# Dealing layer 2's projections to the attention groups in other shares, and summing the shift's part of their biases in layer 1

## Chip, cores and metric

The kernel runs on one core of one Trainium2 chip. The metric is device time in microseconds (us) of one execution, the median of several runs. Shown beside it is one profiled execution, from which every row below is taken.

## What is computed

A model of two layers on 2048 tokens of width 1024 in float32. Layer 1 is gated linear attention (4 heads, chunks). Layer 2 is stick-breaking attention with 16 heads of 64 (8 pairs of heads here) and causal blocks. What enters a projection is normed and modulated: a scale and a shift per channel, both computed from the vector `c`.

```
x = x + gate * gla_mixer(rms_norm(x) * (1 + scale) + shift)              # layer 1
hk = rms_norm(x, kv_gain) * (1 + kv_scale) + kv_shift                    # layer 2
k, v = split(hk @ w_kv)
h = rms_norm(x, norm_gain[1]) * (1 + scale) + shift
q, g = split(h @ sb_w_in)
z = q @ k.T * scale                                                      # per head, s < t only
weights = exp(log_sigmoid(z) + sum over s' in (s, t) of log_sigmoid(-z)) # stick breaking
x = x + gate * ((weights @ v) * silu(g)) @ w_out
y = rms_norm(x)
```

The shift is constant over the tokens, so `shift @ w` is one number per output column, a bias: `bias[f] = sum over d of shift[d] * w[d, f]`.

## The kernel before

Tokens stand in four groups of 512 (`g`). Every matmul operand that needs more than one pass is split into a rounded part (`hi`) and a rest (`lo`); a projection step (`mm3`, L143) is three matmuls of 128x512, and the four projections of one pair and group (`pair_linear`, L732: v, k, q and gate, tiles `lv`, `lk`, `lq`, `lg`) are 33 steps, about 32 x 3 matmuls.

Layer 1 (`layer0`, L661) goes over the groups; side generators started with `spawn` advance one step every so many main steps. The raw halves of all weights, 512 KB each, go through the pool `wraw` of three buffers; ScalarE rounds them (`wh_`), VectorE makes the rest (`wl_`).

Layer 2 (`layer1`, L932) goes over the 8 pairs `p`, and in each over the four groups. Group `g` attends to `g + 1` blocks in two heads, so it has 8, 16, 24 and 32 attention steps. In one step TensorE makes scores `z` (L821, L822); ScalarE a sigmoid `S` (L825); VectorE a running product over `S` (a scan, L830); five steps later TensorE transposes `S` into one of two PSUM banks `pt` (L838); ScalarE and VectorE split it into `sh` and `sl` (L841, L842), which frees the bank; two steps on TensorE multiplies it with the values (`o`, L855, L856). The first four steps of each head are on the diagonal, with narrower tiles.

TensorE's order is the order of the code; the other engines are ordered by a scheduler with priorities, and each then runs its queue in that order. Between attention steps, `step(fill, at)` (L956) advances the projections: during group `g` those of group `g + 1` of the same pair, during the last group those of the next pair's group 0, always 33 steps spread evenly over the stage:

```
elif g + 1 < NG:
    fill.append([pair_linear(p, g + 1, Ws[p], Ls[p]), LIN_STEPS, 0, 1, 0])
```

The weights of the next pair are scaled in `load_scaled` (L121), whose last instructions add the raw weights, times the shift, into `wacc` (L138, L140): 2 x 8 VectorE instructions for a pair. `pair_bias` (L720) sums `wacc` over the partitions with matmuls against ones (`pb`, L725) and copies the result (`wbias`).

Of the kernel before, what the change touches and what calls it, by code (L numbers as in the profile page):

```python
# [34 lines left out]
def yoco_kernel(ctx: ExitStack, tc: tile.TileContext, I: dict, O: dict):  # L35
# [624 lines left out]

    def layer0():  # L661
# [4 lines left out]
        for g in range(NG):  # L666
# [7 lines left out]
            spawn(after, 10, 2)  # L674
            mix, gat = spawn(heads(T)), spawn(gates(T))
# [16 lines left out]
            run(slow)  # L692
            after = normed_out(T)
# [26 lines left out]
    def pair_bias(p, W, i):  # L720
        if W.bias[i] is None:
            pb = bank(pl, f"pb_{p}_{i}")
            W.bias[i] = m2.tile([P, 2], F32, tag="wbias", name=f"wbias_{p}_{i}", bufs=4)
            for j in range(2):
# [3 lines left out]
        return W.bias[i][:, 0:1], W.bias[i][:, 1:2]  # L728
# [3 lines left out]
    def pair_linear(p, g, W, Ls):  # L732
# [14 lines left out]
        bk, bv = pair_bias(p, W, 0)  # L747
# [25 lines left out]
        bq, bgt = pair_bias(p, W, 1)  # L773
# [150 lines left out]

    Ws = {}
# [6 lines left out]
    def layer1(after):  # L932
# [30 lines left out]

        for p in range(SBP):
            for g in range(NG):
# [107 lines left out]
```

## Time and profile before

| what | value |
|---|---|
| median of 3 runs | 2706.71 us (2704.65 to 2706.72) |
| the profiled execution, device time | 2703.88 us |
| its span, first to last instruction | 2702.1 us |
| TensorE (PE) busy | 2607.2 us, 96% |
| weight loads (PEld) busy | 2184.4 us, 81% |
| VectorE (DVE) busy | 2110.4 us, 78% |
| ScalarE (ACT) busy | 1517.6 us, 56% |
| mean granted TensorE clock | 0.989 |

PE's busy time counts each matmul until a modelled end, although the next has begun: the rows of two matmuls in a row overlap. The distance between the starts of two rows is what one really takes. Layer 1 fills the first 976.1 us; pairs 1 to 6 repeat the stages of pair 2, which lie at 1363.6 us (group 0), 1395.5 (1), 1435.1 (2) and 1489.9 to 1556.7 (3). In pair 7 the last group, from 2456.7 us, is filled with the output projection.

### The profile page before, as it was taken

How to read it: one execution, taken by the hardware profiler on the slowest of the kernel's cores; microseconds unless marked ns; L12 is line 12 of the kernel's file. 1: busy time of each engine (PE TensorE's matmuls, PEld its weight loads, DVE VectorE, ACT ScalarE, POOL GpSimd, SP SyncE). 2: the span in 40 equal slices, each digit the busy share in tenths (PEclk: the TensorE clock that was granted, in tenths of full speed). 3: DMA queues.
4: the chain of work that ended last, by engine and by line, in shares of the span. 5: the costliest groups of instructions: out<-in, count | busy, mean ns of one | idle time of the engine just before them, and what ended most of it. 6: DMA issues, size and time to landing. Idle time of an engine off the chain costs nothing.

```text
span 2702.1 us, 38165 instructions
## 1 busy us (share of the span) xinstructions
PE 2607.2 (96%) x14040; PEld 2184.4 (81%) x14040; DVE 2110.4 (78%) x2933; ACT 1517.6 (56%) x2677; POOL 167.4 (6%) x358
## 2 busy tenths in 40 slices
PE   5999999999999999999999999999999999999998
PEld 4888888888788878788787887887887887887887
DVE  7647767676675658978979969979879789789866
ACT  4746756574485445545545645546556555556644
POOL 3000000000000011000010010010000010010000
PEclk7999999999999999999999999999999999999999
DMA  6326445545732463342243334243243243323464
GB/s 246 118 74 209 151 151 175 168 148 173 232 131 72 164 247 127 106 145 90 96 146 116 114 107 154 88 137 116 75 148 110 72 151 113 115 93 117 148 212 147
DMA packets 116682, 371.91 MB, mean 138 GB/s; under 512 B 13872, under 2 KB 18096, under 8 KB 116496
## 3 DMA queue, kind: packets, MB, share of 16 engines
q1 hardware_dynamic: 116496, 369.47, 40.8%
q8 instruction: 111, 1.82, 0.3%
q14 instruction: 75, 0.61, 0.1%
HBM read 311.75 MB, written 40.89 MB: 131 GB/s over the span
## 4 chain that ended last, share of the span: by engine, by line
PE 75%; DVE 17%; ACT 3%; issue 3%; DMA 1%; POOL 0%; SPq 0%; DVEq 0%; POOLq 0%; ACTq 0%
PE pt L838 7%; DVE S L830 5%; PE z L822 4%; PE o L856 4%; PE z L821 4%; PE o L855 3%; DVE sl L842 3%; PE pg L150 2%; PE pg L152 2%; PE pg L151 2%; PE pf L150 2%; PE pf L151 2%; PE pf L152 2%; PE py L150 2%; PE lk L150 2%
## 5 line engine op out<-in xcount | busy, mean ns | idle before, releaser
L841 ACT ACTIVATE sh<-pt 128x512 fp32r<-128x512 f32 (+3 forms) x640 | 341.5, 534 | 531.7 <-PE pt L838 522.1
L842 DVE SCALAR_TENSOR_TENSOR sl<-pt,sh 128x512 fp32r<-128x512 f32 (+3 forms) x640 | 384.0, 601 | 163.5 <-ACT sh L841 157.6
L830 DVE TENSOR_TENSOR_SCAN S<-S,S 128x512 f32<-128x512 f32 x384 | 489.5, 1275 | 3.4 <-ACT S L825 3.0
L838 PE MATMUL pt<-ident,S 128*128 128x128 f32 x2176 | 346.9, 275 | 34.7 <-DVE sl L842 34.2
L838 PEld LDWEIGHTS pt<-ident,S 128*128 128x128 f32 x2176 | 266.1, 141 | 119.7 <-DVE sl L842 33.0
L825 ACT ACTIVATE S<-z 128x512 f32<-128x512 f32 (+3 forms) x640 | 339.5, 531 | 12.6 <-PE o L856 4.6
L821 PE MATMUL z<-k,q 128*128 128x512 f32 (+3 forms) x640 | 284.4, 444 | 0.0
L822 PE MATMUL z<-k,ql 128*128 128x512 f32 (+3 forms) x640 | 234.1, 366 | 0.9 <-DVE sl L842 0.5
L856 PE MATMUL o<-sl,v 128*128 128x512 f32 (+3 forms) x640 | 234.2, 366 | 0.0
L855 PE MATMUL o<-sh,v 128*128 128x512 f32 (+3 forms) x640 | 230.6, 360 | 0.0
L830 DVE TENSOR_TENSOR_SCAN S<-S 128x128 f32<-128x128 f32 (+3 forms) x256 | 209.3, 820 | 19.7 <-POOL S L827 16.7
L827 POOL TENSOR_SCALAR_AFFINE_SELECT S<-S 128x128 f32<-128x128 f32 x256 | 86.1, 337 | 1251.1 <-ACT S L825 1232.2
L444 PE MATMUL pv<-wh_v,h 128*128 128x256 f32 x512 | 155.0, 303 | 0.0
L446 PE MATMUL pv<-wh_v,h 128*128 128x256 f32 x512 | 145.3, 284 | 0.0
L445 PE MATMUL pv<-wl_v,h 128*128 128x256 f32 x512 | 145.2, 284 | 0.0
L855 PEld LDWEIGHTS o<-sh,v 128*128 128x128 f32 x640 | 120.6, 188 | 27.2
L856 PEld LDWEIGHTS o<-sl,v 128*128 128x128 f32 x640 | 120.6, 189 | 25.7
L821 PEld LDWEIGHTS z<-k,q 128*128 128x128 f32 x640 | 121.8, 190 | 5.5
L822 PEld LDWEIGHTS z<-k,ql 128*128 128x128 f32 x640 | 123.1, 192 | 1.5 <-DVE sl L842 0.7
L150 PE MATMUL pg<-h,wh_g 128*128 128x512 f32 x256 | 112.6, 440 | 0.0
L150 PE MATMUL lk<-xb,wh_w_kv 128*128 128x512 f32 x256 | 102.5, 400 | 7.6 <-DVE oB L869 7.6
L150 PE MATMUL lv<-xb,wh_w_kv 128*128 128x512 f32 x256 | 102.9, 402 | 3.5 <-DMA xb<-xn 3.5
(266 smaller groups left out, 6350.3 us busy)
## 6 DMA issues: line engine op xcount, KB each, us to landing
xb<-xn SPq DMA_DIRECT2D x256, 512.0 KB, 5.0
wa_l<-in_w_ada_dram SPq DMA_DIRECT2D x40, 512.0 KB, 5.2
wr_f<-in_w_out_dram SPq DMA_DIRECT2D x40, 512.0 KB, 3.8
x<-in_x_dram SPq DMA_DIRECT2D x32, 512.0 KB, 6.5
wr_v<-in_w_v_dram SPq DMA_DIRECT2D x32, 512.0 KB, 4.5
wr_kq<-in_w_kq_dram SPq DMA_DIRECT2D x32, 512.0 KB, 4.1
wr_g<-in_w_g_dram SPq DMA_DIRECT2D x32, 512.0 KB, 3.9
wr_out<-in_w_out_dram SPq DMA_DIRECT2D x32, 512.0 KB, 3.8
```

The lines of the kernel that those rows point to most:

```text
L150: nc.tensor.matmul(out, hi, x[kt][0], start=first and i == 0, stop=False)
L444: nc.tensor.matmul(o, xh, hi, start=i == 0, stop=False)
L446: nc.tensor.matmul(o, xl, hi, start=False, stop=i == len(steps) - 1)
L821: nc.tensor.matmul(z, L.q[:, h, tcol], k[:, h, 0:w], start=True, stop=False)
L822: nc.tensor.matmul(z, L.ql[h][:, tcol], k[:, h, 0:w], start=False, stop=True)
L825: nc.scalar.activation(s, z, AF.Sigmoid, scale=-SCALE_B)
L830: nc.vector.tensor_tensor_scan(s[:, ::-1], s[:, ::-1], s[:, ::-1], 1.0 if diag else self.before.S[tb][:, 0:1], ALU.mult, ALU.min)
L838: nc.tensor.transpose(pt[:, tb * P:(tb + 1) * P], self.S[tb][:, sb * P:(sb + 1) * P], ident)
L841: nc.scalar.activation(hi, pt[:, t0 * P:], AF.Copy, bias=-1.0)
L842: nc.vector.scalar_tensor_tensor(lo, pt[:, t0 * P:], -1.0, hi.bitcast(F32), op0=ALU.add, op1=ALU.subtract)
L855: nc.tensor.matmul(o, v, hi, start=self.diag and sb == 0, stop=False)
L856: nc.tensor.matmul(o, v, lo, start=False, stop=self.c == 0 and sb == 3)
```

## The change

First, the bias sums move. `load_scaled` loses its sums; the new `bias_sums` runs as a side generator in layer 1 (group index 2 for `w_kv`, 3 for `w_qg`), one half of a weight every 12 main steps. It loads all raw weights of all pairs once more, sums them on VectorE, transposes each sum (`pb`) and adds over the free axis into one small tile `biases`. Second, the projections become one stream over all pairs and groups, in the same order; a group's stage now gets its share by `AHEAD`: after group `g`, the stream is that part of a projection ahead of what the next group needs. Within a pair the stages get 16.5, 29.7, 38 and 47.9 steps, where each had 33. The scaling of the next weights hangs on the stream: `w_qg` of a pair along its own group 0, `w_kv` along the second half of group 3 of the pair before.

```
-                s = b[:, kt:kt + 1]
-                with relaxed(400):
-                    if kt == 0:
-                        nc.vector.tensor_scalar(acc, raw[:, j], s, None, op0=ALU.mult)
-                    else:
-                        nc.vector.scalar_tensor_tensor(acc, raw[:, j], s, acc, op0=ALU.mult, op1=ALU.add)
                 yield
...
+    biases = cpool.tile([P, 4 * SBP], F32, tag="biases", name="biases")
+    def bias_sums(i):
+        which, m = (("w_kv", "kvm"), ("w_qg", "l1m"))[i]
+        b = mods[m][1]
+        def total(p, acc):
+            pb = bank(po, f"pb_{i}_{p}")[:, 0:2 * P]
+            for j in range(2):
+                nc.tensor.transpose(pb[:, j * P:(j + 1) * P], acc[:, j * P:(j + 1) * P], ident)
+            at = 4 * p + 2 * i
+            nc.vector.tensor_reduce(biases[:, at:at + 2], pb.rearrange("p (j t) -> p j t", j=2),
+                                    axis=mybir.AxisListType.X, op=ALU.add)
+        before = None
+        for p in range(SBP):
+            acc = t2(f"bs_{i}_{p}")[:, 0:2 * P]
+            for hf in range(2):
+                raw = wraw.tile([P, 4, 256], F32, tag="wraw", name=f"wb_{i}_{p}_{hf}")
+                nc.sync.dma_start(raw, I[which][p][:, 4 * hf:4 * hf + 4, :])
+                for j in range(4):
+                    kt = 4 * hf + j
+                    s = b[:, kt:kt + 1]
+                    with relaxed(200):
...
+                yield
+            if before:
+                total(*before)
+            before = p, acc
+        yield
+        total(*before)
...
             spawn(after, 10, 2)
+            extra = spawn(bias_sums(g - 2), 10, 12) if g > 1 else iter(())
...
             run(slow)
+            run(extra)
...
-    def pair_bias(p, W, i):
-        if W.bias[i] is None:
-            pb = bank(pl, f"pb_{p}_{i}")
...
-                nc.tensor.matmul(pb[:, j:j + 1], W.acc[:, i, j * P:(j + 1) * P], ones,
-                                 start=True, stop=True)
-            nc.vector.tensor_copy(W.bias[i], pb[:, 0:2])
+    def pair_bias(p, i):
+        at = 4 * p + 2 * i
+        return biases[:, at:at + 1], biases[:, at + 1:at + 2]
...
+    AHEAD = (0.1, 0.0, 0.15, 0.6)
...
+        def projections():
+            for p in range(SBP):
+                for g in range(NG):
+                    side, start, every = iter(()), 0, 2
+                    if g == 0:
+                        if p == 0:
+                            continue
+                        side = pair_weights(p, Ws[p], 1)
+                    elif g == NG - 1 and p + 1 < SBP:
+                        Ws[p + 1] = new_weights(p + 1)
+                        side, start = pair_weights(p + 1, Ws[p + 1], 0), LIN_STEPS // 2
+                    for i, _ in enumerate(pair_linear(p, g, Ws[p], Ls[p])):
+                        if i >= start and (i - start) % every == 0:
+                            next(side, None)
+                        yield
+                    run(side)
+                    yield
+        stream = projections()
+        made = [0]
+        def project(n):
+            while made[0] < n and next(stream, 0) is None:
+                made[0] += 1
...
-                elif g + 1 < NG:
-                    fill.append([pair_linear(p, g + 1, Ws[p], Ls[p]), LIN_STEPS, 0, 1, 0])
...
+                n0, n1 = made[0], int(LIN_STEPS * (NG * p + g + 1 + AHEAD[g]))
...
+                def go(at):
+                    step(fill, at)
+                    project(n0 + int(at * (n1 - n0) + 1e-6))
...
+                project(LIN_STEPS * (NG * p + g + 1))
```

How TensorE's queue changes, in pair 2, group 3, first head: from one pair of scores to the next. Before (one step of three matmuls of the next pair's `lk`):

```order
L150 MATMUL lk_3_0_13865<-xb_3_0_1_13653,wh_w_kv3_0_13359 128x512
L151 MATMUL lk_3_0_13865<-xb_3_0_1_13653,wh_w_kv3_0_13359 128x512
L152 MATMUL lk_3_0_13865<-xb_3_0_1_13653,wl_w_kv3_0_13360 128x512
L855 MATMUL o_2_3_0_3_13850<-sh_2_3_0_3_1_13814,v2_2_3_13594 128x384
L856 MATMUL o_2_3_0_3_13850<-sl_2_3_0_3_1_13815,v2_2_3_13594 128x384
L838 MATMUL pt_2_3_0_2_0_13889<-ident_86,S_2_3_0_2_0_13759 128x128
L838 MATMUL pt_2_3_0_2_0_13889<-ident_86,S_2_3_0_2_1_13782 128x128
L838 MATMUL pt_2_3_0_2_0_13889<-ident_86,S_2_3_0_2_2_13802 128x128
L838 MATMUL pt_2_3_0_2_0_13889<-ident_86,S_2_3_0_2_3_13821 128x128
```

After, the same place; a second projection step stands between the values and the transposes (in every second attention step there), and the stream has reached `lq`:

```order
L142 MATMUL lq_3_0_14081<-xb_3_0_1_13797,wh_w_qg3_0_13817 128x512
L143 MATMUL lq_3_0_14081<-xb_3_0_1_13797,wh_w_qg3_0_13817 128x512
L144 MATMUL lq_3_0_14081<-xb_3_0_1_13797,wl_w_qg3_0_13818 128x512
L879 MATMUL o_2_3_0_3_14085<-sh_2_3_0_3_1_14038,v2_2_3_13749 128x384
L880 MATMUL o_2_3_0_3_14085<-sl_2_3_0_3_1_14039,v2_2_3_13749 128x384
L142 MATMUL lq_3_0_14081<-xb_3_0_2_13799,wh_w_qg3_0_13817 128x512
L143 MATMUL lq_3_0_14081<-xb_3_0_2_13799,wh_w_qg3_0_13817 128x512
L144 MATMUL lq_3_0_14081<-xb_3_0_2_13799,wl_w_qg3_0_13818 128x512
L862 MATMUL pt_2_3_0_2_0_14108<-ident_86,S_2_3_0_2_0_13979 128x128
L862 MATMUL pt_2_3_0_2_0_14108<-ident_86,S_2_3_0_2_1_14001 128x128
L862 MATMUL pt_2_3_0_2_0_14108<-ident_86,S_2_3_0_2_2_14026 128x128
L862 MATMUL pt_2_3_0_2_0_14108<-ident_86,S_2_3_0_2_3_14045 128x128
```

VectorE's queue in pair 2, group 2, second head, off the diagonal. Before:

```order
L830 SCALAR_TENSOR_TENSOR S_2_2_1_1_0_13433<-S_2_2_1_1_0_13433,S_2_2_1_2_0_13319 128x512
L140 SCALAR_TENSOR_TENSOR wacc_3_13028<-wr_w_kv3_1_13519,cond_kv_2178,wacc_3_13028 128x256
L140 SCALAR_TENSOR_TENSOR wacc_3_13028<-wr_w_qg3_0_13712,cond_l1_4112,wacc_3_13028 128x256
L842 SCALAR_TENSOR_TENSOR sl_2_2_0_0_3_13450<-pt_2_2_0_0_3_13444,sh_2_2_0_0_3_13449 128x512
L830 SCALAR_TENSOR_TENSOR S_2_2_1_1_1_13456<-S_2_2_1_1_1_13456,S_2_2_1_2_1_13348 128x512
L140 SCALAR_TENSOR_TENSOR wacc_3_13028<-wr_w_kv3_1_13519,cond_kv_2178,wacc_3_13028 128x256
L140 SCALAR_TENSOR_TENSOR wacc_3_13028<-wr_w_qg3_0_13712,cond_l1_4112,wacc_3_13028 128x256 x2
L842 SCALAR_TENSOR_TENSOR sl_2_2_1_2_0_13473<-pt_2_2_1_2_0_13467,sh_2_2_1_2_0_13472 128x512
```

After, the sums are gone from between the scan and the split; the projection's own `ql` stand there earlier than they did, and four scalings of the next weights' rest in a row:

```order
L854 SCALAR_TENSOR_TENSOR S_2_2_1_1_0_13632<-S_2_2_1_1_0_13632,S_2_2_1_2_0_13528 128x512
L802 SCALAR_TENSOR_TENSOR ql0_2_3_13636<-lq_2_3_13501,biases_124,q_2_3_13635 64x512
L804 SCALAR_TENSOR_TENSOR ql1_2_3_13637<-lq_2_3_13501,biases_124,q_2_3_13635 64x512
L866 SCALAR_TENSOR_TENSOR sl_2_2_0_0_3_13667<-pt_2_2_0_0_3_13661,sh_2_2_0_0_3_13666 128x512
L854 SCALAR_TENSOR_TENSOR S_2_2_1_1_1_13673<-S_2_2_1_1_1_13673,S_2_2_1_2_1_13556 128x512
L866 SCALAR_TENSOR_TENSOR sl_2_2_1_2_0_13689<-pt_2_2_1_2_0_13683,sh_2_2_1_2_0_13688 128x512
L854 SCALAR_TENSOR_TENSOR S_2_2_1_1_2_13695<-S_2_2_1_1_2_13695,S_2_2_1_2_2_13581 128x512
L131 SCALAR_TENSOR_TENSOR wl_w_qg3_1_13959<-wr_w_qg3_1_13956,a_l1_6169,wh_w_qg3_1_13958 128x256 x4
L866 SCALAR_TENSOR_TENSOR sl_2_2_1_2_1_13713<-pt_2_2_1_2_1_13708,sh_2_2_1_2_1_13712 128x384
```

VectorE's queue in layer 1, group 2, at the first weight half of the sums, after (before, none of the rows of L680 and L682 stood there):

```order
L680 TENSOR_SCALAR bs_0_0_4209<-wb_0_0_0_4210,cond_kv_2179 128x256
L117 TENSOR_TENSOR wl_v2_1_1_4292<-wr_v2_1_1_4289,wh_v2_1_1_4291 128x1024
L391 TENSOR_SCALAR gk_2_1_4248<-u_2_1_4246,vecs_97 128x512
L196 TENSOR_TENSOR ss_y1_4207<-ss_y1_4207,sq_y1_1_4228 128x512
L682 SCALAR_TENSOR_TENSOR bs_0_0_4209<-wb_0_0_0_4210,cond_kv_2179,bs_0_0_4209 128x256
L196 TENSOR_TENSOR ss_y1_4207<-ss_y1_4207,sq_y1_2_4243 128x512
L682 SCALAR_TENSOR_TENSOR bs_0_0_4209<-wb_0_0_0_4210,cond_kv_2179,bs_0_0_4209 128x256
L449 TENSOR_TENSOR gk_2_0_4132<-pk_2_0_4295,gk_2_0_4132 128x512
```

The sums of one half are spread among other work of the queue, and the raw half stays in its `wraw` buffer until the last of its four.

## Rows read from the trace of the kernel before

**Rows 1.** The page, part 1: engine, busy us, share of the span, instructions.

```profile
PE 2607.2 (96%) x14040; PEld 2184.4 (81%) x14040; DVE 2110.4 (78%) x2933; ACT 1517.6 (56%) x2677; POOL 167.4 (6%) x358
```

**Rows 2.** Stretches, pair 2: us, then PE, PEld, DVE, ACT, POOL busy, clock, DMA.

```profile
1363.60:1395.50 31.90, 31.90 (x164) 26.57 (x162) 17.72 (x24) 12.00 (x24) 3.70 (x10) 1.00 0.25 70
1395.50:1435.10 39.60, 39.60 (x213) 33.25 (x212) 32.25 (x44) 20.39 (x41) 4.06 (x10) 1.00 0.50 168
1435.10:1489.90 54.80, 51.99 (x281) 42.40 (x279) 51.72 (x81) 34.82 (x71) 3.71 (x10) 1.00 0.34 115
1489.90:1556.70 66.80, 64.40 (x356) 53.33 (x353) 64.86 (x88) 39.77 (x78) 3.57 (x10) 1.00 0.32 106
```

**Rows 3.** Waits of PE in pair 2: us in total, times, longest.

```profile
PE pt L838 <- DVE sl L842: 4.0, 7, 1.2
PE lk L150 <- DVE oB L869: 1.1, 1, 1.1
```

**Rows 4.** Waits of PE from 976.1 to 2456.7 us.

```profile
PE pt L838 <- DVE sl L842: 31.5, 53, 2.3
PE lk L150 <- DVE oB L869: 7.6, 7, 1.1
```

**Rows 5.** Timeline of PE, pair 2, group 2: start, us, instruction, idle before.

```profile
1481.18 0.40 PE L856 MATMUL o<-sl,v 128*128 128x512 f32 x1
1482.74 0.30 PE L838 MATMUL pt<-ident,S 128*128 128x128 f32 x1 [1.17 <-DVE sl L842]
```

**Rows 6.** Timeline of DVE there.

```profile
1482.04 0.56 DVE L842 SCALAR_TENSOR_TENSOR sl<-pt,sh 128x384 fp32r<-128x384 f32 x1
1482.51 0.48 DVE L140 SCALAR_TENSOR_TENSOR wacc<-wr_w_qg,cond_l,wacc 128x256 f32<-128x256 f32 x1
1482.90 1.28 DVE L830 TENSOR_TENSOR_SCAN S<-S,S 128x512 f32<-128x512 f32 x1
1484.10 0.66 DVE L869 TENSOR_TENSOR oB<-o,ot 64x512 f32<-64x512 f32 x1
```

**Rows 7.** Timeline of PE, pair 2, early in group 3.

```profile
1507.04 0.39 PE L152 MATMUL lv<-xb,wl_w_kv 128*128 128x512 f32 x1
1507.28 0.38 PE L838 MATMUL pt<-ident,S 128*128 128x128 f32 x2
1507.41 0.48 PE L821 MATMUL z<-k,q 128*128 128x512 f32 x1
1507.73 0.39 PE L822 MATMUL z<-k,ql 128*128 128x512 f32 x1
...
1508.42 0.50 PE L725 MATMUL pb<-ones,wacc 128*128 128x1 f32 x4
1510.05 0.50 PE L150 MATMUL lk<-xb,wh_w_kv 128*128 128x512 f32 x1 [1.13 <-DVE oB L869]
```

**Rows 8.** DVE groups by line, 976.1 to 2456.7: busy us, mean ns | idle before.

```profile
L780 DVE SCALAR_TENSOR_TENSOR ql<-lq,wbias,q 64x512 fp32r<-64x512 f32 x31 | 23.5, 757 | 0.9
L140 DVE SCALAR_TENSOR_TENSOR wacc<-wr_w_qg,cond_l,wacc 128x256 f32<-128x256 f32 x49 | 23.4, 477 | 0.8
...
L727 DVE COPY wbias<-pb 128x2 f32<-128x2 f32 x14 | 1.9, 136 | 0.0
```

**Rows 9.** Busy time by stretch, layer 1: groups 2 and 3.

```profile
498.30:730.30 232.00, 228.57 (x1281) 195.33 (x1280) 164.98 (x223) 140.32 (x211) 3.86 (x4) 0.99 0.53 176
730.30:976.10 245.80, 245.63 (x1339) 208.24 (x1340) 146.79 (x224) 134.54 (x212) 4.23 (x6) 0.99 0.41 140
```

**Rows 10.** Waits of the DMA queue on SP from 498.3 to 976.1 us, the longest.

```profile
SPq L106 <- DVE wl_out L117: 66.9, 13, 12.0
```

**Rows 11.** The page, part 6: DMA issues, KB each, us to landing.

```profile
wr_v<-in_w_v_dram SPq DMA_DIRECT2D x32, 512.0 KB, 4.5
```

**Rows 12.** DVE groups by line, layer 1, group 2.

```profile
L117 DVE TENSOR_TENSOR wl_out<-wr_out,wh_out 128x1024 fp32r<-128x1024 f32 x8 | 9.8, 1219 | 2.4 <-ACT wh_out L116 2.4
```

More of the change, by code (lines that the diff above doesn't have):

```diff
@@ L119, in load_split, with load_scaled @@
         return out
-    def load_scaled(name, src, out, mod, acc):
-        a, b = mod
+    def load_scaled(name, src, out, a):
         for hf in range(2):
@@ L659, in is_ready @@
         yield
+    biases = cpool.tile([P, 4 * SBP], F32, tag="biases", name="biases")
[19 more added lines that the diff above has]
+                    with relaxed(200):
+                        if kt == 0:
+                            nc.vector.tensor_scalar(acc, raw[:, j], s, None, op0=ALU.mult)
+                        else:
+                            nc.vector.scalar_tensor_tensor(acc, raw[:, j], s, acc, op0=ALU.mult, op1=ALU.add)
+                yield
[4 more added lines that the diff above has]
+        total(*before)
     def layer0():
@@ L709, in new_weights @@
         W = Piece()
-        W.acc = t2(f"wacc_{p}").rearrange("p (i f) -> p i f", i=2)
-        W.w, W.bias = {}, [None, None]
+        W.w = {}
         return W
@@ L717, in pair_weights @@
         W.w[which] = []
-        return load_scaled(f"{which}{p}", I[which][p], W.w[which], mods[m], W.acc[:, i])
-    def pair_bias(p, W, i):
-        if W.bias[i] is None:
-            pb = bank(pl, f"pb_{p}_{i}")
-            W.bias[i] = m2.tile([P, 2], F32, tag="wbias", name=f"wbias_{p}_{i}", bufs=4)
-            for j in range(2):
-                nc.tensor.matmul(pb[:, j:j + 1], W.acc[:, i, j * P:(j + 1) * P], ones,
-                                 start=True, stop=True)
-            nc.vector.tensor_copy(W.bias[i], pb[:, 0:2])
-        return W.bias[i][:, 0:1], W.bias[i][:, 1:2]
+        return load_scaled(f"{which}{p}", I[which][p], W.w[which], mods[m][0])
+    def pair_bias(p, i):
+        at = 4 * p + 2 * i
+        return biases[:, at:at + 1], biases[:, at + 1:at + 2]
     LIN_STEPS = 4 * KT + 1
@@ L746, in pair_linear @@
         yield from mm3(pv, W.w["w_kv"], 1, xs)
-        bk, bv = pair_bias(p, W, 0)
+        bk, bv = pair_bias(p, 0)
         vt = t2(f"vt_{n}")
@@ L772, in pair_linear @@
         yield from mm3(pq, W.w["w_qg"], 0, xs)
-        bq, bgt = pair_bias(p, W, 1)
+        bq, bgt = pair_bias(p, 1)
         L.q = t4(f"q_{n}", [P, 2, TG], F32R)
@@ L975, in layer1 @@
                     fill.append([finals, FINAL_STEPS + SBP - 1, 0, 1.0, 0])
-                elif g + 1 < NG:
-                    fill.append([pair_linear(p, g + 1, Ws[p], Ls[p]), LIN_STEPS, 0, 1, 0])
-                elif p + 1 < SBP:
-                    fill.append([pair_weights(p + 1, Ws[p + 1], 1), KT, 0, 0.6, 0])
-                    fill.append([pair_linear(p + 1, 0, Ws[p + 1], Ls[p + 1]), LIN_STEPS, 0, 1, 0])
-                if g == 2 and p + 1 < SBP:
-                    Ws[p + 1] = new_weights(p + 1)
-                    fill.append([pair_weights(p + 1, Ws[p + 1], 0), KT, 0.5, 1, 0])
+                n0, n1 = made[0], int(LIN_STEPS * (NG * p + g + 1 + AHEAD[g]))
                 steps = [(u, j) for u in units for j in range(4)]
+                def go(at):
+                    step(fill, at)
+                    project(n0 + int(at * (n1 - n0) + 1e-6))
                 for i, (u, j) in enumerate(steps):
@@ L987, in layer1 @@
                     turns.append((u, j))
-                    step(fill, (i + 0.7) / len(steps))
+                    go((i + 0.7) / len(steps))
                     if len(values) > LAG_V:
@@ L991, in layer1 @@
                         v[0].values(v[1])
-                    step(fill, (i + 1) / len(steps))
+                    go((i + 1) / len(steps))
                     if len(turns) > LAG_T:
```

## Prediction

> **What bounds the kernel now.** The page comes first, and it misleads: TensorE is busy 96% of the span [rows 1], so nothing seems to be left but TensorE's own work, of which this change removes next to nothing. The second view is the busy time by stage in one pair of layer 2 [rows 2]. There the reader is to see two regimes. In groups 0 and 1 TensorE is never idle and VectorE is busy 56% and 81% of the stage. In groups 2 and 3 VectorE is busy 94% and 97%, and TensorE loses 2.8 and 2.4 us. The third view says to whom [rows 3]: in each pair seven transposes wait for `sl`, the VectorE instruction that frees a `pt` bank, 4.0 us, and one `lk` waits 1.1 us for a PSUM bank until `oB` is done. Over pairs 0 to 7, up to the start of the last group, that is 53 times and 31.5 us, and 7 times and 7.6 us [rows 4]; 7 x 7 of the 53 are pairs 0 to 6.
>
> The idle column is too small. In [rows 5] the value matmul starts at 1481.18 and the transpose that waits at 1482.74, 1.56 us later; a matmul of this size otherwise gives way after 0.24 us (from 1507.04 to 1507.28 in [rows 7]). The loss is 1.32 us, and the row says 1.17: some 0.16 us of each such wait lies under the modelled end of the matmul ahead. So a pair loses 4.0 + 7 x 0.16 + 1.1 = 6.2 us.
>
> Why `sl` is late stands in VectorE's queue [rows 6]: a sum into `wacc` runs ahead of a 1.28 us scan, and holds the queue from 1482.51 to 1482.90. One attention step off the diagonal costs VectorE a scan and an `sl`, whatever group it is in; one projection step costs TensorE 3 x 0.23 = 0.70 us and VectorE little. Groups 2 and 3 have most of the attention and no more projection than the others: too little for TensorE to do while VectorE catches up.
>
> **The change, part by part.**
>
> *Sums out of layer 2.* 16 instructions of 0.477 us [rows 8] leave VectorE in each of seven pairs: 7.6 us a pair, nearly all in groups 2 and 3. They are worth what they delay, so they are counted with the waits, next.
>
> *Projections dealt anew.* Groups 2 and 3 get 38 + 47.9 steps instead of 66: 19.9 x 0.70 = 13.9 us of TensorE's work move there from groups 0 and 1. Groups 2 and 3 last 121.6 us; without 6.2 of waits and 1.0 of `pb` (below), and with 13.9 more, TensorE needs 128.3. VectorE's 116.6 there lose 7.6 and gain 0.6 of a projection's seven instructions at up to 0.757 us [rows 8], 3.2: 112.2 us, 87% of the stage where it was 96%. Groups 0 and 1 keep 57.6 us of TensorE and 46.8 of VectorE, 81%, no more than group 1 has now without a wait. So TensorE becomes the bound in every group, and a pair lasts what TensorE needs. What stays of the 6.2 us: nothing, if 87% is as harmless as 81%; 2.7 us, if the loss grows in proportion between 81% and 96%. I take 1.0, because waits arise only once VectorE has fallen behind by the two steps that the two `pt` banks cover; the order shows the densest place, the second head of group 2, without its sums but still with scaling of weights. Seven pairs: 43.4 us of waits (7 x 6.2) come down to 7. The `lk` wait is in that sum: it arises where `pb` takes a bank besides `lv` and two `o`, and `pb` is gone from there.
>
> The Trainium skill (Perfetto Trace Analysis, Identifying the Most-Contended Engine) holds TensorE's busy share to be a poor measure of its headroom, matmuls being pipelined, and wants the weight loads' share instead. By the rows that share is 83% and 84% in groups 0 and 1, and 77% and 80% in groups 2 and 3 [rows 2], which agrees that something is lost there. At the 84% of group 1, groups 2 and 3 would need 50.5 and 63.5 us, 7.6 less a pair; by idle time alone it would be 5.2. The sum goes by the 6.2 of the waits.
>
> *`pb` out of layer 2.* In [rows 7] `lk` starts 1.63 us after `pb`, of which 1.13 is the wait: one `pb` group costs 0.50 us. There are 16, two of them at the end of layer 1: -8.0 us.
>
> *`pb` in layer 1.* 16 pairs of transposes. Two cost 0.13 us until the next matmul starts, and that one gives way after 0.32 instead of 0.23 us [rows 7]: 0.22 x 16 = +3.5 us.
>
> *Sums in layer 1.* Per pair and weight, eight sums of 0.477 and a reduction, which no row shows. Its bounds are the 0.136 us copy and the 0.757 us `ql` [rows 8]; I take 0.4, nearer to the middle because it reads 256 columns. 4.2 us x 8 = 34 us of VectorE in group 2 and in group 3. Group 2 goes from 165 to 199 busy us of 232, 86%; group 3 from 147 to 173 of 246, with the first pair's 7.6 gone [rows 9]. The cover is TensorE, which lacks 3.4 and 0.2 us in these groups. If it were gone, 86% could cost what 94% costs in layer 2, 2.8 of 54.8 us, or 12 us for group 2. I take 2, within 0 to 12. The 32 loads add 8.4 MB a group at 176 and 140 GB/s [rows 9].
>
> *Pair 7.* Four of the 53 waits are there, beside the first weights of the output projection. Its group 2 keeps 33 steps and loses no sums, so those waits stay; VectorE comes to it with nothing less to do: +2 (0 to 4).
>
> *ScalarE* is busy 60 to 64% in groups 2 and 3 [rows 2]; its instructions only move. *The DMAs* of the stream (`xb`, `w_qg`, `w_kv`) are issued at the same place of the stream as before, on the same queue.
>
> **Sum**, against the profiled execution: 2703.9 - 43.4 + 7 - 8.0 + 3.5 + 2 + 2 = 2667. The median of the runs shown is 2.8 us above that execution, the lowest run 0.8; I leave that inside the range. A change of under 0.2% (5.4 us) can't be told from none here.
>
> **The rivals.**
>
> *All of the loss goes.* TensorE's need, as the weight loads give it, is reached in all seven pairs, and layer 1 waits nowhere: 2703.9 - 7 x 7.6 - 8.0 + 3.5 = 2646. The Trainium skill's measure, above, points here. For it: groups 0 and 1 show no wait at all. Against: the second head of group 2 stays close.
>
> *VectorE stays the limit in lumps.* Scaling of weights and the projection's own splits come in bursts of four and two and still stand ahead of `sl`; half of the 43.4 stays: 2703.9 - 21.7 - 8.0 + 3.5 + 2 + 2 = 2682. For it: the longest waits of a pair lie at such bursts, `ql` among them. Against: the mean load falls by nine points.
>
> *It does nothing.* The waits move with the stream, for another bank or for `xb`, and only `pb` is won: 2703. For it: TensorE's 96%. Against: [rows 3], where the waits name VectorE.
>
> *Slower, by the raw buffers of layer 1.* Three `wraw` buffers now take 72 loads in group 2 instead of 56. A half holds its buffer for 4.5 us of landing [rows 11] and two splits; VectorE's takes 1.22 us [rows 12], and ScalarE's is taken as no longer, so 6.9 us in all, an estimate. 56 of these are 386 of 3 x 232 = 696 buffer-us; the 16 new halves may hold theirs 19.4 us each before buffers run out. Their four sums are spread over the queue; if they held 29 us, 154 buffer-us would be missing, 51 us of the group, and the time would be 2716. It decides from about 28 us on. For it: the loads already wait on SP for buffers, 66.9 us for `wl_out` alone [rows 10], and what waits there holds the loads behind it. Against: the order puts the last sum of the first half some 15 rows of 0.5 to 1.2 us after its first, 10 to 14 us.
>
> **Chances.** Forecast 0.53; all goes 0.15; half stays 0.20; nothing 0.06; slower 0.06. Faster by over 0.2%: 0.88. From 2645 to 2692 the range holds the forecast with its bounds (2656 to 2691: residue 0 to 19, layer 1 0 to 12, pair 7 0 to 4), the half case and the full one.
>
> **What would show it.** Right: in pair 2, groups 2 and 3 together at 128 to 130 us, groups 0 and 1 at 57 to 58, `pt <- sl` under 1.5 us a pair, no `lk <- oB`; layer 1's groups 2 and 3 longer by 2 to 4 us each. Wrong: `pt <- sl` still 2 us or more a pair (the half case), a new name in TensorE's waits of layer 2, or layer 1 longer by more than 12 us, with waits for `wl_` weights.

## The result and the profile after

The changed kernel takes 2678.49 us (median of 4 runs, 2674.69 to 2679.87); the kernel before, run beside it, 2705.68 us. The ratio is 0.9903, with a 95% interval of 0.9891 to 0.9915: 27 us less where 37 were forecast. The time lies in the range, but it is the sum of two misses: layer 2 gave more than forecast, and layer 1 took much more. The profiled execution took 2677.76 us, its span is 2676.1 us. The page still shows TensorE at the top of part 1, as in [rows 1]:

```profile
PE 2595.5 (97%) x14008; PEld 2184.6 (82%) x14008; DVE 2127.7 (80%) x2933; ACT 1519.0 (57%) x2677; POOL 171.4 (6%) x358
```

Where the time went is seen by cutting the span at the first scores `z` of pair 0 (end of layer 1), of each stage of layer 2, and at the first low-rank gate matmul `plr` of each group of layer 1:

| stretch | before, us | after, us |
|---|---|---|
| layer 1, group 1 | 227.5 | 230.1 |
| layer 1, group 2 (sums of `w_kv`) | 232.0 | 247.3 |
| layer 1, group 3 (sums of `w_qg`) | 245.8 | 255.6 |
| end of layer 1 | 976.1 | 1003.4 |
| pair 0 | 194.3 | 200.4 |
| a pair, 1 to 6 | 193.1 | 185.6 |
| pair 7 with the output projection | 373.2 | 358.9 |
| layer 2 in all (span less end of layer 1) | 1726.0 | 1672.7 |

Layer 2 is 53.3 us shorter, layer 1 is 27.3 us longer. Group 1, which no part of the change touches, came out at 227.3 to 230.3 us in the fourteen profiles of this study, so some 2.6 of the 27.3 are likely no effect of it. The pairs 1 to 6 repeat within 0.4 us in both kernels. Pairs 0 and 7 do not: in the kernels below that build layer 2 as the whole change does, layer 2 takes 1672.7 to 1676.5 us, so its total gain is 49 to 53 us, and differences of up to 4 us in it mean nothing.

The stretches of pair 2 answer to [rows 2] (us, then PE, PEld, DVE, ACT, POOL busy, clock, DMA):

```profile
1389.40:1410.30 20.90, 20.90 (x115) 17.53 (x113) 15.91 (x22) 10.66 (x21) 2.74 (x8) 1.00 0.58 207
1410.30:1447.80 37.50, 37.50 (x203) 31.50 (x202) 30.65 (x43) 19.83 (x41) 3.95 (x10) 1.00 0.31 107
1447.80:1501.40 53.60, 53.60 (x291) 44.91 (x290) 50.29 (x74) 36.10 (x75) 3.90 (x10) 1.00 0.44 154
1501.40:1575.00 73.60, 73.28 (x392) 60.90 (x391) 65.21 (x80) 40.27 (x76) 5.54 (x12) 1.00 0.22 76
```

TensorE is now busy throughout, and its weight loads fill 84%, 84%, 84% and 83% of the four stages. VectorE is at 0.94 of group 2, as before the change, and yet TensorE waits for it nowhere there. The waits of PE in this pair answer to [rows 3], one row instead of two:

```profile
PE pt L862 <- DVE sl L866: 0.3, 1, 0.3
```

Over 1003.4 to 2433.9 us, the stretch of [rows 4], it is 10 waits instead of 53 (5.3 of their 7.2 us in pair 7, which has no projections of a next pair; it had 3.2 us before). A new name is a wait of `lv` in pair 0 for `g`, the VectorE instruction that empties a projection's bank; in the kernel before an `lv` of pair 0 waited 3.5 us for its DMA:

```profile
PE pt L862 <- DVE sl L866: 7.2, 10, 2.0
PE lv L142 <- DVE g L823: 3.1, 1, 3.1
```

Layer 1 is where the rest went. Its groups 2 and 3 by stretch, as in [rows 9]; VectorE has 27.4 and 21.4 us more in them:

```profile
500.40:747.80 247.40, 233.66 (x1298) 198.27 (x1297) 192.33 (x295) 140.28 (x211) 2.63 (x4) 0.97 0.58 198
747.80:1003.40 255.60, 246.50 (x1348) 209.47 (x1349) 168.22 (x278) 135.73 (x213) 5.06 (x6) 0.98 0.50 168
```

and the waits of PE in both. The same list for the kernel before has 0.3 us of `ms_o` and no `ms_y`. No weight is among the names:

```profile
PE ms_o L211 <- DVE ss_o L196: 18.2, 3, 9.1
PE ms_y L211 <- DVE ss_y L196: 3.2, 1, 3.2
PE py L142 <- DVE rq_x L217: 1.0, 1, 1.0
```

`ms_o` is the mean of squares of a head's output `po`: ScalarE squares the two halves (`ss_o`, `sq_o`), VectorE adds them into `ss_o`, TensorE sums them over the partitions. It stands at a fixed place of TensorE's program, and in the kernel before TensorE waited 0.2 us for it in the first head of groups 2 and 3 each: there was no slack. Of the 18.2 us, 7.4 and 9.1 lie there, the rest in a later head. In the first head of group 2 now (timeline of PE: start, us, instruction, idle before):

```profile
569.91 0.28 PE L438 MATMUL pv<-wh_v,h 128*128 128x256 f32 x1
577.55 2.08 PE L211 MATMUL ms_o<-ss_o,mean_v 128*128 128x512 f32 x2 [7.37 <-DVE ss_o L196]
578.64 1.20 PE L436 MATMUL pv<-wh_v,h 128*128 128x256 f32 x1
579.64 0.42 PE L437 MATMUL pv<-wl_v,h 128*128 128x256 f32 x1
```

What ScalarE and VectorE did meanwhile (timelines; `x` and `x1n` are the division of the group before by its norm and its split, which run here as a side generator):

```profile
571.15 1.23 ACT L222 ACTIVATE x1n<-x 128x512 fp32r<-128x512 f32 x2 [1.49 <-DVE x L576]
573.89 0.63 ACT L222 ACTIVATE x1n<-x 128x512 fp32r<-128x512 f32 x1 [1.50 <-DVE x L576]
574.42 0.58 ACT L192 ACTIVATE ss_o<-po 128x512 f32<-128x512 f32 x1
```

```profile
573.17 0.68 DVE L576 TENSOR_TENSOR x<-x,r_y 128x512 f32<-128x512 f32 x1
573.78 1.21 DVE L117 TENSOR_TENSOR wl_kq<-wr_kq,wh_kq 128x1024 fp32r<-128x1024 f32 x1
574.91 0.68 DVE L223 TENSOR_TENSOR x1n<-x,x1n 128x512 fp32r<-128x512 f32 x1
575.51 0.34 DVE L680 TENSOR_SCALAR bs<-wb,cond_kv 128x256 f32<-128x256 f32 x1
575.89 1.00 DVE L682 SCALAR_TENSOR_TENSOR bs<-wb,cond_kv,bs 128x256 f32<-128x256 f32 x2
576.81 0.69 DVE L196 TENSOR_TENSOR ss_o<-ss_o,sq_o 128x512 f32<-128x512 f32 x1
```

The last matmul of `po` ended at 565.9 us, so the squares could have run from then on; they ran from 574.42, behind all eight splits, the last three of which waited for VectorE. The addition then stood behind a weight split, the last `x1n` and three sums. In the kernel before, ScalarE had the same pieces in another order at this place, the squares ahead of the last three splits. ScalarE got no work by the change, and still its order changed:

```profile
558.17 2.18 ACT L230 ACTIVATE x1n<-x 128x512 fp32r<-128x512 f32 x4
560.25 1.04 ACT L116 ACTIVATE wh_kq<-wr_kq 128x1024 fp32r<-128x1024 f32 x1
561.20 0.58 ACT L200 ACTIVATE ss_o<-po 128x512 f32<-128x512 f32 x1
...
563.15 1.23 ACT L230 ACTIVATE x1n<-x 128x512 fp32r<-128x512 f32 x2 [0.89 <-DVE x L584]
```

So the theory to test was: layer 1 lost its time not to the busy time of the sums but to the order of two queues (ScalarE's and VectorE's), which the scheduler fixed anew once the sums were in. The Trainium skill (Perfetto Trace Analysis, Tensor Engine Instruction (MATMUL, LD_WEIGHTS)) says that VectorE and ScalarE take their instructions strictly first in, first out; these rows agree with it.

### The profile page after: what moved, and what is told of

Read it like the earlier page. It is cut to its first block, busy times and chain, and to the rows that moved or that the text cites. A ratio compares the mean times of both kernels' runs of the same rounds, so it can differ in the third digit from the quotient of the medians.

```text
span 2676.1 us, 38236 instructions
## 1 busy us (share of the span) xinstructions
PE 2595.5 (97%) x14008; PEld 2184.6 (82%) x14008; DVE 2127.7 (80%) x2933; ACT 1519.0 (57%) x2677; POOL 171.4 (6%) x358
## 4 chain that ended last, share of the span: by engine, by line
PE 82%; DVE 8%; ACT 5%; DMA 4%; issue 1%; SPq 0%; DVEq 0%; ACTq 0%
PE pt L862 9%; PE o L880 5%; PE z L846 5%; PE o L879 5%; PE z L845 5%; PE lq L142 2%; PE lk L142 2%; PE lg L142 2%; PE lk L143 2%; PE lk L144 2%; PE lg L143 2%; PE lq L143 2%; PE lg L144 2%; PE lq L144 2%; PE pf L142 2%; PE pf L143 2%
## 5 line engine op out<-in xcount | busy, mean ns | idle before, releaser
L436 PEld LDWEIGHTS pv<-wh_v,h 128*128 128x128 f32 x512 | 99.9, 195 | 7.0 <-issue 2.8
```

What stands on the lines that cost most here:

```text
L436: nc.tensor.matmul(o, xh, hi, start=i == 0, stop=False)
```

## The experiments

Each ratio is against runs of the kernel before on the same chip, with its 95% interval. The whole change has 0.9903 (0.9891 to 0.9915).

### The two parts by themselves

The dealing alone keeps `load_scaled`, `wacc` and `pb` of the kernel before and takes `projections`, `AHEAD` and `project` from the change. 

> The dealing alone: projections as one stream with the new shares, the bias sums left in layer 2 beside the scaling. Theory (the dealing brings most of layer 2's gain, the sums in the first layer cost what the first layer lost): the first layer ends at 976 us again; the sums now fall into group 2 (VectorE was at 0.94 of 53.6 us there, 3.8 us more) and group 3, so a pair is 1 to 2 us longer than with the whole change and the 16 `pb` groups cost 0.5 us each: 2662 to 2675 us. Rival (taking the sums out of layer 2 is what frees it): 2690 to 2703 us.

The sums alone are the changed kernel with the stages of the kernel before:

```
...
-                n0, n1 = made[0], int(LIN_STEPS * (NG * p + g + 1 + AHEAD[g]))
+                elif g + 1 < NG:
+                    fill.append([pair_linear(p, g + 1, Ws[p], Ls[p]), LIN_STEPS, 0, 1, 0])
...
```

> The sums moved to the first layer, the projections dealt evenly as before. Theory: the first layer ends at 1003 us as in the whole change, layer 2 gives back 8 us of `pb` and 2.5 to 4 us of waits a pair: 2690 to 2705 us, about the time of the kernel before. Rival (the dealing is worth nothing beside the sums' removal): 2675 to 2682 us.

Dealing alone: 2688.98 us, ratio 0.9944 (0.9931 to 0.9956). Sums alone: 2686.54 us, ratio 0.9937 (0.9923 to 0.9950). Both expectations were wrong in size, and in the same way: more of layer 2's gain belongs to the sums than the theory had it.

| | end of layer 1, us | layer 2, us | a pair, us |
|---|---|---|---|
| before | 976.1 | 1726.0 | 193.1 |
| dealing alone | 977.1 | 1708.0 | 190.5 |
| sums alone | 1001.8 | 1683.0 | 187.2 |
| both | 1003.4 | 1672.7 | 185.6 |

The dealing alone is held up by the sums: with the stream, 15 of a pair's 16 sums, of both weights, come in the second half of group 2 (from 1461.2 us on), and VectorE is at 0.95 there. Its longest wait, 2.1 us, stands behind three scalings and three sums. The stretch of pair 2's group 2 and the waits of that pair:

```profile
1430.70:1488.40 57.70, 54.37 (x293) 44.65 (x291) 54.96 (x86) 34.96 (x71) 4.36 (x10) 1.00 0.41 143
```

```profile
PE pt L838 <- DVE sl L842: 3.3, 2, 2.1
```

With the sums alone, the projections still dealt evenly, VectorE stays at 0.97 of group 3 (64.7 us), and of the seven waits three are left:

```profile
1500.30:1565.00 64.70, 63.27 (x348) 52.47 (x346) 62.77 (x81) 39.82 (x78) 4.51 (x10) 1.00 0.30 101
```

```profile
PE pt L862 <- DVE sl L866: 1.6, 3, 1.2
```

The two parts go at the same waits: 18.0 and 43.0 us apart (the 43.0 hold the `pb` groups too), 53.3 together. And the sums alone have the whole loss of layer 1, 25.7 us; the dealing has none of it.

### Where in layer 1 the sums lose: time, buffers, load

Two edits of the whole change. In the first the sums start later:

```
-            extra = spawn(bias_sums(g - 2), 10, 12) if g > 1 else iter(())
+            extra = spawn(bias_sums(g - 2), 64, 11) if g > 1 else iter(())
```

> The whole change, with the sums of a group started after its first 64 steps (when the division of the group before by its norm is through) and dealt every 11 steps instead of every 12 from step 10: same work, same loads, same buffers. Theory (the loss of the first layer is the meeting of the sums with that normalisation in the first head of groups 2 and 3, on queues that keep their order): the waits for `ss_o` and `ss_y` of 22 us go, the first layer ends at 978 to 988 us, time 2652 to 2664 us. Rival (VectorE's 27 us of added work in a group, or the raw buffers, wherever they stand): the waits move to later heads, time 2670 to 2682 us.

In the second the raw halves of the sums leave the three shared buffers:

```
-                raw = wraw.tile([P, 4, 256], F32, tag="wraw", name=f"wb_{i}_{p}_{hf}")
+                raw = t4(f"wb_{i}_{p}_{hf}", [P, 4, 256])
```

> The whole change, with the raw halves of the sums in the pool of 14 larger buffers (activations) instead of the three raw buffers that the projections' weights use. Rival of the theory (the three raw buffers: weights come late because a sum holds a buffer): the waits for `ss_o` and `ss_y` go, 2652 to 2664 us. Theory (the meeting of the sums with the normalisation on VectorE's queue): at least half of the waits stay, 2666 to 2680 us.

Late sums: 2690.02 us, ratio 0.9948 (0.9935 to 0.9960), slower than the whole change. The theory in the form "they meet the normalisation" fell. Two waits for `ss_o` stayed, from 566.7 and 824.7 us: the first sums stood ahead of the addition in VectorE's queue at just that place, and the squares again behind all the splits. A new wait came at the end of group 2, where the modulation's rows `aa_l` must be done; that the sums, now dealt closer, caused it was not tested:

```profile
PE ms_o L211 <- DVE ss_o L196: 11.2, 2, 6.2
PE pc_l L242 <- DVE aa_l L236: 11.0, 1, 11.0
```

Own buffers: 2681.6 us, ratio 0.9918 (0.9904 to 0.9931), no better than the whole change. The waits in the two first heads are still there, 7.1 and 5.7 us where they were 7.4 and 9.1, so the raw buffers are not their main cause. The second row is a new wait; it names `a_l`, but `pb` reads a sum, and that sum's last instruction ended at 721.25 us, 0.15 before `pb` started:

```profile
PE ms_o L211 <- DVE ss_o L196: 12.8, 2, 7.1
PE pb L664 <- DVE a_l L263: 5.7, 1, 5.7
```

Next, load against order. The first kernel leaves three quarters of the sums out and keeps all loads:

```
-                        else:
+                        elif j == 0:
                             nc.vector.scalar_tensor_tensor(acc, raw[:, j], s, acc, op0=ALU.mult, op1=ALU.add)
```

> The whole change with all 32 loads of raw halves, but only the first of the four rows of each half is summed (the second half's sum keeps its first row too), so the biases are not the reference's and VectorE has three quarters of the sums' 57 us less to do. In its queues the squares `ss_o` of the first head stand behind all eight splits `x1n` in groups 2 and 3, as with the whole change. Theory (what PE waits for is the place of `ss_o` in ScalarE's and VectorE's queues, which the sums only shifted): waits of 3 to 7 us for `ss_o` stay in both groups, 2666 to 2674 us. Rival (the sums' busy time on VectorE): three quarters of the first layer's 25 us come back, 2656 to 2662 us.

The second keeps all work and changes the order, with a lower priority for the division and the split:

```
+            with relaxed(400 if g in (1, 2) else 0):
                 nc.vector.tensor_tensor(T.x1[f], T.x1[f], r, op=ALU.mult)
             xn = tact(f"x1n_{g}_{f}")
+            with relaxed(400 if g in (1, 2) else 0):
                 split(xn[:, 0], xn[:, 1], T.x1[f])
```

> The whole change, with the eight divisions and splits `x`, `x1n` of the normalisation given a lower priority in groups 2 and 3, so that the squares `ss_o` stand ahead of `x1n` 1 to 7 (group 2) and 4 to 7 (group 3) in ScalarE's queue; same work, same loads. Theory (the place in the queue): the waits for `ss_o` fall under 2 us each, the first layer ends at 983 to 992 us, 2658 to 2668 us. Rival (VectorE has too much to do there): as much wait turns up at other names of the first head, 2674 to 2680 us.

A quarter of the sums: 2672.0 us, ratio 0.9887 (0.9872 to 0.9903). With VectorE's busy time in group 2 down from 192.3 to 173.1 us, at 0.71 of the group as before the change, the wait is still there, 7.6 us in group 2 and 6.8 in group 3 (a third, of 1.5, is in a later head). Layer 1 ends at 996.6 us, so three quarters of the sums' work are worth 6.7 of the 27.3 us there:

```profile
PE ms_o L211 <- DVE ss_o L196: 15.8, 3, 7.6
```

Squares first: 2664.59 us, ratio 0.9860 (0.9848 to 0.9873). All sums are there, and the wait is gone in group 2 and 1.6 us in group 3. Layer 1 ends at 987.4 instead of 1003.4 us; group 3, at 246.3 us, is 0.5 longer than before the change, with eight pairs' sums in it. Of the 16.0 us the whole kernel keeps some 12, by the ratios and by the spans: its pairs 0 and 7 are 1.0 and 2.7 us longer, within the spread given above. Group 2 keeps 8.9 us, spread over small waits at several names. The largest of them, and then the `ms_o` of group 3:

```profile
PE ms_y L211 <- DVE ss_y L196: 3.2, 1, 3.2
PE ms_o L211 <- DVE ss_o L196: 1.6, 1, 1.6
```

The wait for `ss_y`, the same sum of squares for the group's output, shows an order again. In the kernel before its last five additions run as one block; with squares first they start at 537.15, 538.89, 539.75, 542.36 and 543.56 us, with a weight split, sums, a copy and a row of `aa_l` between them. The block before:

```profile
534.70 3.88 DVE L204 TENSOR_TENSOR ss_y<-ss_y,sq_y 128x512 f32<-128x512 f32 x5 [0.38 <-ACT sq_y L203]
```

The reverse is the sharpest test: the kernel before, with no sums moved and no dealing, and only a lower priority for the squares and the addition `ss_o` of two heads. ScalarE's squares kept their place ahead of the last three splits; VectorE's addition moved back.

```
-        with urgent():
+        with relaxed(200) if T.g > 1 and h == 0 else urgent():
             ss = result(sumsq_steps(f"o{n}", pos))
```

> The kernel before, without any part of the change, in which the addition of the squares `ss_o` of the first head of groups 2 and 3 has a lower priority, so that it stands on VectorE behind all the splits `x1n` and two weight splits, about as with the whole change; no work is added. Theory (the place in the queue by itself makes PE wait): waits of 4 to 7 us for `ss_o` in both groups and 1 us each at a lower clock behind them, 2712 to 2720 us against 2703. Rival (it takes the sums' load): the time of the kernel before within 3 us.

It took 2722.34 us, ratio 1.0065 (1.0051 to 1.0079): 18 us slower than the kernel before by the ratio, 20 by the medians, with no work added. Group 2 has 241.5 us instead of 232.0, group 3 253.2 instead of 245.8, with VectorE as busy as before (165.3 and 147.1 us). PE's waits in them, and what the addition stood behind:

```profile
PE ms_o L219 <- DVE ss_o L204: 11.1, 2, 6.1
```

```profile
568.63 1.28 DVE L244 SCALAR_TENSOR_TENSOR aa_l<-wa_l,s_col,aa_l 128x1024 f32<-128x1024 f32 x1
569.83 1.22 DVE L117 TENSOR_TENSOR wl_g<-wr_g,wh_g 128x1024 fp32r<-128x1024 f32 x1
570.96 0.69 DVE L204 TENSOR_TENSOR ss_o<-ss_o,sq_o 128x512 f32<-128x512 f32 x1
```

So a place in VectorE's queue alone makes a loss of this kind, and it needs no load. Layer 1 got 17.0 us longer for 10.8 us more of `ms_o` waits; TensorE was also busy 3.4 and 2.6 us longer in the two groups with the same instructions, at a mean granted clock of 0.97 and 0.98 instead of 0.99 (last section).

### The sums on another engine, and in another place

On GpSimd, as a multiplication and an addition for each row:

```
...
-                            nc.vector.scalar_tensor_tensor(acc, raw[:, j], s, acc, op0=ALU.mult, op1=ALU.add)
...
+                        nc.gpsimd.tensor_scalar(raw[:, j], raw[:, j], s, None, op0=ALU.mult)
+                        nc.gpsimd.tensor_tensor(acc, acc, raw[:, j], op=ALU.add)
```

> The whole change, with the bias sums on GpSimd as a multiplication and an addition per row (240 instructions of 128x256), VectorE free of them. The squares `ss_o` stand ahead of `x1n` 5 to 7 (group 2), 6 and 7 (group 3). Theory (place in the queue and VectorE's load both gone): the first layer ends at 979 to 990 us, 2655 to 2666 us. Rival (the raw buffers: an engine at 1 to 2 us a row holds each for 8 to 16 us, and the weights of the projections come late): new waits of PE for `wl_` or `wh_` weights, 2680 us and more.

In layer 2, in the pair before:

```
...
+                if g < 2 and p + 1 < SBP:
+                    fill.append([bias_sums(p + 1, g), 4, 0, 1, 0])
```

> The change with the sums of a pair's biases made in layer 2 in the pair before, from halves loaded again, in group 0 (keys and values) and group 1 (queries and gate), where VectorE is busy 0.76 of 21.0 us and 0.82 of 37.5 us; only pair 0's stand in the first layer, in group 3 from step 100 on. Theory (the sums cost only where they meet work that PE waits for): the first layer ends at 976 to 980 us, a pair is 0.4 to 1 us longer than with the whole change for its two `pb`, 2652 to 2662 us. Rival (VectorE is the limit in groups 0 and 1 too once it has 3.8 us more): 3 us a pair and more, 2672 us and more.

On GpSimd: 2710.19 us, ratio 1.0036 (1.0024 to 1.0048), some 36 us behind the whole change by the ratios. In the profiled execution, the slowest of the six (2717.8 us), layer 1 ends at 1042.1 us. Neither theory had it in full: a row costs GpSimd 1.17 and 0.89 us where VectorE took 0.48, so raw buffers are held longer, as the rival said, but no weight is among the names that PE waits for in layer 1's groups 2 and 3. Most of the time goes to VectorE (`ss_o` 25.3 us in five, `psc` for `e` 9.9 us in three). A new name is GpSimd itself, which masks `sc` for `po`; at the longest of these waits three multiplications of the sums stood ahead of the mask (from 863.29 us, 2.73 us):

```profile
PE po L493 <- POOL sc L474: 10.7, 5, 3.9
```

VectorE's own instructions got longer too. Groups of VectorE by line in group 2, first the whole change, then this kernel:

```profile
L196 DVE TENSOR_TENSOR ss_y<-ss_y,sq_y 128x512 f32<-128x512 f32 x7 | 4.8, 682 | 0.0
L563 DVE SCALAR_TENSOR_TENSOR x<-py,cond_g,x 128x512 f32<-128x512 f32 x8 | 5.9, 743 | 2.1 <-PE py L144 2.1
```

```profile
L196 DVE TENSOR_TENSOR ss_y<-ss_y,sq_y 128x512 f32<-128x512 f32 x7 | 6.2, 880 | 0.8 <-ACT sq_y L195 0.3
L563 DVE SCALAR_TENSOR_TENSOR x<-py,cond_g,x 128x512 f32<-128x512 f32 x8 | 5.9, 746 | 1.5 <-PE py L144 1.5
```

In the pairs: 2669.08 us, ratio 0.9878 (0.9865 to 0.9891), some 7 us better than the whole change by the ratios, and less than expected. Layer 1 ends at 971.9 us, somewhat earlier than theory had it (976 to 980), but a pair takes 188.0 us, 2.4 more than with the whole change and near the rival's 3. Group 0 takes the sums for 0.2 us, with VectorE at 0.90; group 1 does not, 2.6 us longer at 0.89, for waits of `pt`:

```profile
1364.40:1385.60 21.20, 21.20 (x119) 17.78 (x117) 19.11 (x32) 10.75 (x21) 2.88 (x8) 1.00 0.62 214
1385.60:1425.70 40.10, 38.12 (x207) 31.69 (x204) 35.50 (x55) 21.56 (x45) 4.87 (x10) 1.00 0.49 161
```

```profile
PE pt L852 <- DVE sl L856: 2.0, 2, 1.7
```

### A better version

The sums of `w_qg` in layer 1's group 3 with the squares first, those of `w_kv` in group 0 of the pair before, none in layer 1's group 2:

```
...
-            extra = spawn(bias_sums(g - 2), 10, 12) if g > 1 else iter(())
+            extra = spawn(chain(bias_sums(0, 0), *(bias_sums(p, 1) for p in range(SBP))), 10, 6) if g == 3 else iter(())
...
+                if g == 0 and p + 1 < SBP:
+                    fill.append([bias_sums(p + 1, 0), 4, 0, 1, 0])
```

> A version put together from the runs so far: the dealing kept; the query and gate sums of all pairs in the first layer's group 3 (VectorE was busy 0.60 of it before), with the splits of the normalisation at lower priority there so that `ss_o` stands ahead of `x1n` 2 to 7; the key and value sums of a pair in group 0 of the pair before (a group with 2.9 us of sums more was 0.2 us longer in the last run), none in the first layer's group 2 but pair 0's in group 3. Theory (what the sums cost is decided by what they meet): group 2 of the first layer at 229 to 232 us, group 3 at 246 to 249 us, a pair 0.2 to 0.5 us longer than with the whole change, 2650 to 2660 us. Rival (the sums cost by their busy time wherever they are): 2664 us and more.

2664.99 us, ratio 0.9858 (0.9844 to 0.9871). That is the rival's time (2664 and more), and no better than squares first alone. Layer 1's group 2 is 228.7 us and a pair 185.3, as expected or better, but group 3 is 256.9: the total of the first sum was asked for too early.

```profile
762.76 0.66 PE L676 MATMUL pb<-ident,bs 128*128 128x128 f32 x2 [8.59 <-ACT kf L410]
```

```profile
760.57 2.04 DVE L671 SCALAR_TENSOR_TENSOR bs<-wb,cond_kv,bs 128x256 f32<-128x256 f32 x4
```

The row names ScalarE's `kf` as releaser, but `pb` reads only the sum. The four sums of the second half end at 762.61, and `pb` starts 0.15 us later: it waited for them. The next kernel asks for a total only after the next sum's two halves (`before = gen` in a loop over the sums, started at step 30, every 10 steps); the one beside it has `AHEAD = (0.0, 0.0, 0.0, 0.0)` as well.

> As the last version, but the total of a sum (the two transposes `pb`) is asked for on PE only after the next sum's two halves, and the sums start at step 30 of the first layer's group 3, one half every 10 steps; the last version had lost 8.6 us in one wait of PE for the first sum there. Theory (a sum costs by what stands behind it): that wait goes, group 3 at 246 to 250 us, 2648 to 2657 us. Rival: the wait moves to another name of group 3, 2660 to 2667 us.

> The same kernel with even shares (every stage gets the next stage's 33 steps, no projections ahead): what the dealing is worth when the sums are nowhere in the way. By the two runs that differ only in the dealing with the sums in the first layer (layer 2 at 1683.0 and 1672.7 us) it should be 8 to 13 us slower than the kernel beside it, 2657 to 2670 us. Rival (the dealing is worth nothing without the sums in layer 2): within 3 us of it.

With the lag: 2661.85 us, ratio 0.9846 (0.9831 to 0.9861), 42 us under the kernel before and some 15 under the whole change by the ratios. It is the lowest ratio of the study, but its interval overlaps those of squares first and of the version above. And it is the rival's time: the wait for `pb` is gone, and one of 5.4 us for `ss_o` is back, ended at 802 us. Its squares were done at 797.1, and four sums, `x1n` and the two products `e` and `b` stood ahead of the addition in VectorE's queue; one of the sums waited 0.9 us for its raw half. Group 3 has 253.8 us.

```profile
PE ms_o L211 <- DVE ss_o L196: 5.4, 1, 5.4
```

With even shares: 2670.39 us, ratio 0.9874 (0.9858 to 0.9891). The dealing is worth 8.5 us here, as the expectation had it (8 to 13), and 1.4 us a pair (186.7 against 185.3), much as between the sums alone and the whole change (1.6 us a pair).

## Why the prediction was right and wrong

**Layer 2: the mechanism right, the size low.** Groups 2 and 3 together are 127.2 us (signs given: 128 to 130), groups 0 and 1 58.4 (57 to 58), `pt <- sl` 0.3 us a pair (under 1.5), no `lk <- oB`. The term that was mis-sized is "seven pairs: 43.4 us of waits come down to 7". A pair forecast at 6.2 us less (6.2 of waits, 1.0 of `pb`, less 1.0 of residue) lost 7.5. Of the residue 0.3 us of idle time is left, and the other 0.6 us is loss that no row of waits showed; the measure by weight loads, which stood beside the sum as 7.6, was the nearer one. Layer 2 as a whole was forecast 41.4 us shorter (43.4 - 7 + 14 x 0.50 for `pb` - 2) and is 53.3. Six pairs of 7.5 give 45; pair 0 is 6.1 longer, but has 0.6 of a projection more by `AHEAD` (0.6 x 33 x 0.70 = 13.9 us by the step's price), and pair 7 is 14.3 shorter with as much less. Pair 7's waits for `sl` grew by 2.1 us, as the term of 2 had it. One of the signs of being wrong did appear, a new name in TensorE's waits of layer 2 (`lv` for `g`, 3.1 us, once in pair 0), but it is no part of what a pair lost or won.

One reading of the rows was wrong. In [rows 6] the sum into `wacc` runs behind the `sl` that ended the wait of 1.17 us, so it can't have held it up. What stood ahead of that `sl` were two `ql` of the projection itself:

```profile
1480.50 0.72 DVE L778 SCALAR_TENSOR_TENSOR ql<-lq,wbias,q 64x512 fp32r<-64x512 f32 x1
1481.25 0.76 DVE L780 SCALAR_TENSOR_TENSOR ql<-lq,wbias,q 64x512 fp32r<-64x512 f32 x1
```

Sums did stand ahead of an `sl` in the wait before it (0.75 us, ended at 1479.54; three sums from 1477.41 on), and the runs of each part show that taking them out frees most of layer 2. So the mechanism stands, but by other rows than the one shown.

**The premise about busy shares failed.** The residue was taken from VectorE's share, 87% forecast for groups 2 and 3 together. It came out at 91% (115.5 of 127.2 us), in group 2 at 0.94 as before, without a wait. In these rows the share does not tell whether TensorE waits; what stands ahead of `sl` does. In group 1 of the run with the sums in the pairs VectorE was at 0.89, and TensorE waited 2.0 us.

**The dealing and the sums were never priced apart.** The prediction counted the 16 sums "with the waits". Apart, the sums' removal is worth 43.0 us in layer 2 and the dealing 18.0, 10.3 on top of the sums.

**Layer 1: the step that failed** is "I take 2, within 0 to 12" for the sums there. With the two `pb` terms layer 1 was forecast 4.5 us longer (2 + 3.5 - 2 x 0.50) and is 27.3; groups 2 and 3 are 15.3 and 9.8 us longer where the sign said 2 to 4 each. That the total lies in the range is luck: layer 2's surplus of some 12 us paid for half of layer 1's miss. Its argument went by VectorE's share of group 2 (86% forecast, 78% measured) and by the raw buffers, and it took the price of a busy share from layer 2. The size of the work was right: 0.48 us a sum, 0.41 us a reduction. What was missed is that the scheduler puts two queues in a new order when work is added, and that TensorE's `ms_o` had a slack of nothing: ScalarE's squares moved behind the last three splits, VectorE's addition behind those too and behind weight splits and sums. Two heads lost 7.4 and 9.1 us at that one wait. Moving only the order in the changed kernel took 16.0 us out of layer 1; making only the order in the kernel before put 17.0 us into it. The sign given for a wrong prediction, "longer by more than 12 us, with waits for `wl_` weights", came true in its first half only. With the squares first 11.2 us stay in layer 1, 8.9 of them in group 2, where VectorE is at 0.80. The largest wait there, 3.2 us for `ss_y`, again shows an order; how much of the 8.9 is order and how much load was not tested, and stays open.

**The rivals.** "All of the loss goes" was right for the pairs of layer 2 and wrong for layer 1. "Half stays" has nearly the right total (2682) for a wrong reason: a pair of layer 2 kept 0.3 us of its waits. "Slower, by the raw buffers" falls with the run with other buffers, and no weight is among TensorE's waits.

## What to carry to other kernels

Work added to an engine with a fixed queue can cost more by what it pushes back than by its busy time: before a price is put on it, compare the built order of each queue before and after at the places where TensorE waited with no slack, also on an engine that got no new work (ScalarE here). An order that the scheduler happens to pick can be worth nearly as much as the change itself (18 to 20 us here, by one priority), so fix it with priorities and measure the change again. And price two edits that go at the same waits apart and together: 18.0 and 43.0 us made 53.3.

## What the runs showed of the hardware

Waits of TensorE cost more than their length here. After the 7.4 us of idle time in the changed kernel's group 2 the granted clock was 0.50 of full speed, that is the lower of the two levels, 1.2 GHz, for at least 3.5 us:

```profile
578.50:582.00 3.50, 3.50 (x13) 2.57 (x12) 0.53 (x1) 2.30 (x3) 0.00 (x0) 0.50 0.96 332
```

A `pv` matmul gave way after 0.22 us there (579.64 to 579.86), and after 0.12 before the wait (569.79 to 569.91). In the kernel with late squares group 2 got 9.5 us longer for 6.0 us more of that wait, and group 3 7.4 for 4.7.

GpSimd at work made VectorE slower, but not all of it: with the sums on GpSimd an addition with both inputs in SBUF (`ss_y`) rose from 682 to 880 ns, one that reads PSUM (`x<-py`) stayed at 743 and 746. The Trainium skill (SBUF — State Buffer, Who interferes with whom) says just this, that a VectorE instruction with two SBUF inputs contends with GpSimd instructions that read SBUF; the two rows agree.
